# Row normalization by absolute sum: loads and stores on two queues, the last tile in halves, one broadcast multiply per tile

## The chip, the cores and the metric

The kernel runs on one core of a Trainium2 chip. The metric is the device time of the whole kernel in microseconds; the time before is the median of 8 runs. A profiled execution of the same kernel gives the busy times, waits and transfers that this document reads. Engines are named as in the profile: DVE is VectorE, ACT is ScalarE, POOL is GpSimd, SP is SyncE, and "SPq" is SP's queue of DMA issues.

## The reference

The input is 32 x 512 x 1024 in f32, that is 16384 rows of 1024. Each row is divided by the sum of its absolute values:

```python
def reference(x):
    sums = np.sum(np.abs(x), axis=-1, keepdims=True)
    return (x / (sums + 1e-8)).astype(np.float32)
```

67.1 MB are read and 67.1 MB are written, and nothing is used twice.

## The kernel before

The 16384 rows are cut into 8 tiles of 2048 rows. In a tile each of the 128 partitions holds R = 16 whole rows that lie one behind the other in memory, so a tile is 128 x 16 x 1024 f32: 64 KB per partition, 8.39 MB in all. The pool `sbuf` has three buffers for `x_tile`, so three tiles can be on the chip at a time, and a tile is computed in place: the buffer that was loaded is also the one that is stored, and it is free for the next load when its store has landed.

For each tile one DMA loads it (line 66, on SP's queue). `process_chunk` then works on a number of rows per partition: VectorE sums the absolute values along each row (`tensor_reduce`, line 37) and takes the reciprocal (line 45). The rows are then multiplied by their reciprocals one instruction per row, the first `mv` rows by VectorE (`tensor_scalar_mul`, line 48), the others by ScalarE (`activation` with a scale, line 54). The chunk is then stored by a DMA on SP's queue too (line 60).

The first six tiles are one chunk of 16 rows, with 10 rows on VectorE and 6 on ScalarE. The last two tiles are loaded whole but computed and stored in four chunks of 4 rows, with 2 rows on each engine; these stores are 2 MB each.

Loads and stores stand in one queue, SP's, and the tile framework's scheduler decides their order. In the trace it is: loads of tiles 0, 1, 2; stores of 0, 1, 2; loads of 3, 4, 5; stores of 3, 4, 5; loads of 6 and 7; the eight 2 MB stores. A store that waits for its rows holds up the loads behind it on SP. On VectorE the scheduler interleaves the chunks of the last two tiles.

Of the kernel before, what the change touches and what calls it, by code (L numbers as in the profile page):

```python
# [1 line left out]

# [4 lines left out]


@with_exitstack  # L10
def kernel(
    ctx: ExitStack,
    tc: tile.TileContext,
    x: bass.AP,
    out: bass.AP,
):
    nc = tc.nc
    P = nc.NUM_PARTITIONS

    x_flat = x.flatten_outer_dims()  # L20
    out_flat = out.flatten_outer_dims()
    n, d = x_flat.shape

    R = 16
    assert n % (P * R) == 0
    ntiles = n // (P * R)

    x_t = x_flat.rearrange("(n p r) d -> n p r d", p=P, r=R)
    out_t = out_flat.rearrange("(n p r) d -> n p r d", p=P, r=R)

    BUFS = 3
    sbuf = ctx.enter_context(tc.tile_pool(name="sbuf", bufs=BUFS))
    stats = ctx.enter_context(tc.tile_pool(name="stats", bufs=BUFS))

    def process_chunk(x_tile, out_ap, r0, rN, mv):
        s = stats.tile([P, rN], mybir.dt.float32, tag="s")
        nc.vector.tensor_reduce(  # L37
            out=s[:, :],
            in_=x_tile[:, r0 : r0 + rN, :],
            axis=mybir.AxisListType.X,  # L40
            op=mybir.AluOpType.add,
            apply_absolute_value=True,
        )
        inv = stats.tile([P, rN], mybir.dt.float32, tag="inv")
        nc.vector.reciprocal(out=inv[:, :], in_=s[:, :])  # L45
        for r in range(rN):
            if r < mv:
                nc.vector.tensor_scalar_mul(  # L48
                    out=x_tile[:, r0 + r, :],
                    in0=x_tile[:, r0 + r, :],  # L50
                    scalar1=inv[:, r : r + 1],
                )
            else:
                nc.scalar.activation(  # L54
                    out=x_tile[:, r0 + r, :],
                    in_=x_tile[:, r0 + r, :],
                    func=mybir.ActivationFunctionType.Copy,
                    scale=inv[:, r : r + 1],
                )
        nc.sync.dma_start(out=out_ap[:, r0 : r0 + rN, :], in_=x_tile[:, r0 : r0 + rN, :])  # L60

    MV = 10

    for i in range(ntiles):
        x_tile = sbuf.tile([P, R, d], x.dtype)
        nc.sync.dma_start(out=x_tile[:, :, :], in_=x_t[i, :, :, :])

        if i < ntiles - 2:
            process_chunk(x_tile, out_t[i], 0, R, MV)
        else:  # L70
            C = 4
            for c0 in range(0, R, C):
                process_chunk(x_tile, out_t[i], c0, C, (MV * C) // R)


# [1 line left out]
_INS = ['x']  # L77
_OUTS = [((32, 512, 1024), 'float32')]


# [23 lines left out]
```

## Time and profile before

| | |
|---|---|
| median of 8 runs | 318.69 us (318.1 to 319.26) |
| profiled execution | 319.0 us |
| its span on the core | 317.2 us |
| VectorE busy | 190.8 us, 60% of the span |
| ScalarE busy | 56.6 us, 18% |
| HBM read and written | 67.11 MB each, 423 GB/s over the span |
| DMA packets | 3170, of which 352 under 512 B |
| VectorE waited for loads | 111.5 us, 3 times |

Times in the profile are counted from the start of the span. The share of a DMA queue is the time that its packets took on the core's 16 DMA engines, as a share of 16 engines' span. A transfer's "time to landing" runs from the start of its issue on the queue to the last of its 16 completion marks, so it includes the transfers that stand ahead of it in the queue. "Idle before" of a group is the time that the engine stood still just before the group's instructions, with what ended it.

### The profile page before, as it was taken

The page shows a single profiled execution, that of the slowest core. Times are in us where ns is not written, and L with a number is a line of the kernel's source. Part 1 is how long each engine was busy: PE and PEld are TensorE (multiplying, and loading weights), DVE is VectorE, ACT ScalarE, POOL GpSimd, SP SyncE. Part 2 cuts the span into 40 slices and gives each one's busy share as a digit, 9 for nine tenths or more (in the row PEclk, how much of TensorE's full clock was granted, in tenths as well). Part 3 has the DMA queues.
Part 4 walks back from the last instruction along what each step waited for, and adds up shares of the span by engine and source line. Part 5 has one row for each costly group of instructions (what it writes and reads, how often), then busy time and mean ns, then how long its engine had stood idle before and what let it go on. Part 6 is the DMA issues. An engine that isn't in the chain of part 4 may idle for free.

```text
span 317.2 us, 261 instructions
## 1 busy us (share of the span) xinstructions
DVE 190.8 (60%) x104; ACT 56.6 (18%) x53; POOL 0.2 (0%) x4
## 2 busy tenths in 40 slices
DVE  0019999999990000039999999980000069999920
ACT  0010080080080000000070070080000002522520
POOL 0000000000000000000000000000000000000000
DMA  9999999999999999999999999999999999999797
GB/s 388 405 397 471 455 397 405 388 438 479 405 397 521 405 397 430 488 405 397 512 413 397 397 480 438 405 438 471 413 397 479 438 405 438 390 433 430 326 430 331
DMA packets 3170, 134.24 MB, mean 423 GB/s; under 512 B 352, under 2 KB 352, under 8 KB 352
## 3 DMA queue, kind: packets, MB, share of 16 engines
q1 hardware_dynamic: 3168, 134.22, 98.5%
q14 instruction: 2, 0.02, 0.0%
HBM read 67.11 MB, written 67.11 MB: 423 GB/s over the span
## 4 chain that ended last, share of the span: by engine, by line
DVE 56%; DMA 35%; issue 4%; ACT 0%; ACTq 0%; SPq 0%; DVEq 0%
DVE s L37 41%; DMA x_tile<-in_x_dram 35%; DVE x_tile L48 15%; DVE inv L45 1%; ACT x_tile L54 0%; ACTq L99 0%; SPq L60 0%; DVEq L45 0%; DVEq L48 0%
## 5 line engine op out<-in xcount | busy, mean ns | idle before, releaser
L37 DVE TENSOR_REDUCE s<-x_tile 128x4 f32<-128x4096 f32 (+1 forms) x14 | 138.3, 9892 | 111.5 <-DMA x_tile<-in_x_dram 111.5
L54 ACT ACTIVATE x_tile<-x_tile,inv 128x1024 f32<-128x1024 f32 x52 | 55.4, 1137 | 224.1 <-DVE inv L45 224.1
L48 DVE TENSOR_SCALAR x_tile<-x_tile,inv 128x1024 f32<-128x1024 f32 x76 | 51.4, 747 | 0.3
L54 ACT ACT_TABLE_LOAD x1 | 1.3, 1283 | 23.0 <-DMA x_tile<-in_x_dram 23.0
L45 DVE RECIPROCAL inv<-s 128x4 f32<-128x4 f32 (+1 forms) x14 | 2.7, 202 | 0.4
L88 POOL MEMSET const-bfloat16-1.0<- 128x1 bf16 x1 | 0.1, 101 | 0.0
L88 POOL MEMSET const-uint8-127<- 128x1 uint8 x1 | 0.1, 101 | 0.0
L88 POOL MEMSET const-float32-0.0<- 128x1 f32 x1 | 0.1, 98 | 0.2 <-issue 0.2
L88 POOL MEMSET const-float32-1.0<- 128x1 f32 x1 | 0.1, 98 | 0.0
## 6 DMA issues: line engine op xcount, KB each, us to landing
out_dram<-x_tile SPq DMA_DIRECT2D x8, 2048.0 KB, 9.9
x_tile<-in_x_dram SPq DMA_DIRECT2D x8, 51.1
out_dram<-x_tile SPq DMA_DIRECT2D x6, 29.7
```

Source lines behind the costliest of these rows:

```text
L37: nc.vector.tensor_reduce(out=s[:, :], in_=x_tile[:, r0 : r0 + rN, :], axis=mybir.AxisListType.X, op=mybir.AluOpType.add, apply_absolute_v ...
L45: nc.vector.reciprocal(out=inv[:, :], in_=s[:, :])
L48: nc.vector.tensor_scalar_mul(out=x_tile[:, r0 + r, :], in0=x_tile[:, r0 + r, :], scalar1=inv[:, r : r + 1],)
L54: nc.scalar.activation(out=x_tile[:, r0 + r, :], in_=x_tile[:, r0 + r, :], func=mybir.ActivationFunctionType.Copy, scale=inv[:, r : r + 1],)
L88: nc = _bacc.Bacc("TRN2", target_bir_lowering=False, num_devices=1)
```

## The change

- All stores are issued from ScalarE's queue instead of SP's; loads stay on SP's.
- The loop is put under `manual_schedule`: every engine's instructions keep the order in which the program writes them.
- Tiles 0 to 6 are one chunk of 16 rows. Only the last tile is cut, into two halves of 8 rows, and its load is cut as well; the second-last tile is no longer cut.
- VectorE multiplies half of a chunk's rows (8 of 16, or 4 of 8) by one `tensor_mul`, whose second operand is `inv` broadcast along the row; ScalarE has the other half, one instruction per row as before.
- A step of VectorE adds 1e-8 to the sums ahead of the reciprocal.
- The pool `stats` has four buffers instead of three.

```diff
-    BUFS = 3
     sbuf = ctx.enter_context(tc.tile_pool(name="sbuf", bufs=BUFS))
-    stats = ctx.enter_context(tc.tile_pool(name="stats", bufs=BUFS))
+    stats = ctx.enter_context(tc.tile_pool(name="stats", bufs=4))
 
-    def process_chunk(x_tile, out_ap, r0, rN, mv):
+    def normalize(x_tile, r0, k, kv):
...
+        nc.vector.tensor_scalar_add(out=s[:, :k], in0=s[:, :k], scalar1=EPS)
+        inv = stats.tile([P, R], FP32)
+        nc.vector.reciprocal(out=inv[:, :k], in_=s[:, :k])
+        nc.vector.tensor_mul(
+            out=x_tile[:, r0 : r0 + kv, :],
+            in0=x_tile[:, r0 : r0 + kv, :],
+            in1=inv[:, :kv].unsqueeze(2).to_broadcast([P, kv, d]),
+        )
+        for r in range(kv, k):
+            row = x_tile[:, r0 + r, :]
+            nc.scalar.activation(
+                out=row,
+                in_=row,
+                func=mybir.ActivationFunctionType.Copy,
+                scale=inv[:, r : r + 1],
+            )
+
+    with tc.manual_schedule():
+        for i in range(ntiles):
+            parts = 2 if i == ntiles - 1 else 1
+            k = R // parts
+            x_tile = sbuf.tile([P, R, d], FP32)
+            for r0 in range(0, R, k):
+                nc.sync.dma_start(
+                    out=x_tile[:, r0 : r0 + k, :], in_=x_t[i][:, r0 : r0 + k, :]
                 )
...
+            for r0 in range(0, R, k):
+                normalize(x_tile, r0, k, k // 2)
+                nc.scalar.dma_start(
+                    out=out_t[i][:, r0 : r0 + k, :], in_=x_tile[:, r0 : r0 + k, :]
                 )
...
-        nc.sync.dma_start(out=out_ap[:, r0 : r0 + rN, :], in_=x_tile[:, r0 : r0 + rN, :])
```

On the engines this gives: VectorE runs reduce, add, reciprocal and multiply of one tile after the other, with no interleaving of chunks. ScalarE runs eight rows and a store issue for each tile, and four rows and a store issue for each half of the last. SP issues only the loads; from the fourth on, each waits until the store of the tile that had its buffer has landed.

More of the change, by code (lines that the diff above doesn't have):

```diff
@@ L7 @@
 from concourse._compat import with_exitstack
+FP32 = mybir.dt.float32
+EPS = 1e-8
 @with_exitstack
@@ L26 @@
     ntiles = n // (P * R)
+    BUFS = 3
     x_t = x_flat.rearrange("(n p r) d -> n p r d", p=P, r=R)
     out_t = out_flat.rearrange("(n p r) d -> n p r d", p=P, r=R)
-    BUFS = 3
     sbuf = ctx.enter_context(tc.tile_pool(name="sbuf", bufs=BUFS))
-    stats = ctx.enter_context(tc.tile_pool(name="stats", bufs=BUFS))
-    def process_chunk(x_tile, out_ap, r0, rN, mv):
-        s = stats.tile([P, rN], mybir.dt.float32, tag="s")
+    stats = ctx.enter_context(tc.tile_pool(name="stats", bufs=4))
+    def normalize(x_tile, r0, k, kv):
+        s = stats.tile([P, R], FP32)
         nc.vector.tensor_reduce(
-            out=s[:, :],
-            in_=x_tile[:, r0 : r0 + rN, :],
+            out=s[:, :k],
+            in_=x_tile[:, r0 : r0 + k, :],
             axis=mybir.AxisListType.X,
@@ L43, in process_chunk @@
         )
[L44 to L51, printed above, removed]
-                )
[L53 to L58, printed above, removed]
-                )
@@ L60, in process_chunk @@
[L60 to L73, printed above, removed]
+        nc.vector.tensor_scalar_add(out=s[:, :k], in0=s[:, :k], scalar1=EPS)
```

## The prediction

> **What bounds the kernel now.** I read the page first (busy shares, the DMA row, the chain), then the groups kept apart by shape, then the issue of every transfer and its time to landing, one window at a time.
>
> ```profile
> DMA  9999999999999999999999999999999999999797
> q1 hardware_dynamic: 3168, 134.22, 98.5%
> DVE 56%; DMA 35%; issue 4%; ACT 0%; ACTq 0%; SPq 0%; DVEq 0%
> ```
>
> The chain names VectorE for 56% of the span, and that misleads. The chain goes back through what each instruction waited for last, and while VectorE works on a tile the queue behind it is full all the same: the 16 DMA engines are at nine tenths in all slices but two of the last three, 98.5% over the span. The kernel moves 134.2 MB in 317.2 us. So time goes or comes only where the DMA engines idle or slow down, and where the last transfer lands.
>
> To see how evenly they run I take issue plus time to landing for single transfers (first fence: issue start and its duration; second: the same transfers' time to landing, in the same order).
>
> ```profile
> 0.73 0.38 SPq L66 DMA_DIRECT2D x_tile<-in_x_dram  x1
> 1.64 0.42 SPq L66 DMA_DIRECT2D x_tile<-in_x_dram  x1
> 47.29 0.35 SPq L60 DMA_DIRECT2D out_dram<-x_tile  x1
> 95.98 0.52 SPq L66 DMA_DIRECT2D x_tile<-in_x_dram  x1
> 120.92 0.33 SPq L66 DMA_DIRECT2D x_tile<-in_x_dram  x1
> 164.61 0.34 SPq L60 DMA_DIRECT2D out_dram<-x_tile  x1
> 213.47 0.81 SPq L66 DMA_DIRECT2D x_tile<-in_x_dram  x1
> 303.80 0.33 SPq L60 DMA_DIRECT2D out_dram<-x_tile  x1
> ```
>
> ```profile
> x_tile<-in_x_dram SPq DMA_DIRECT2D x1, 22.2
> x_tile<-in_x_dram SPq DMA_DIRECT2D x1, 61.2
> out_dram<-x_tile SPq DMA_DIRECT2D x1, 34.9
> x_tile<-in_x_dram SPq DMA_DIRECT2D x1, 44.2
> x_tile<-in_x_dram SPq DMA_DIRECT2D x1, 58.7
> out_dram<-x_tile SPq DMA_DIRECT2D x1, 34.3
> x_tile<-in_x_dram SPq DMA_DIRECT2D x1, 43.4
> out_dram<-x_tile SPq DMA_DIRECT2D x1, 2048.0 KB, 12.5
> ```
>
> Write Lk and Sk for load and store of tile k. The sums: L0 lands at 22.9, L2 at 62.8, S0 at 82.2, L3 at 140.2, L5 at 179.6, S3 at 198.9, L6 at 256.9, the last quarter of S7 at 316.3. From S3 to L6 lie three transfers (S4, S5, L6) in 58.0 us: 19.33 us each, 434 GB/s, for loads and stores alike, and S0 to L3 gives the same (58.0 for three). This is the clean price of 8.39 MB. Against it the trace loses: 1.2 us between L0 and L2 (39.9 for two), 0.7 between L3 and L5 (39.4 for two), and 1.3 behind L7, which lands at 276.3 (issued at 218.3; the two loads of that stretch have a median of 50.7, so 58.0 for it): 40.0 for the last two stores instead of 38.7. Sum: 22.9 + 15 x 19.33 + 3.2 = 316.1, measured 316.3; the span ends 0.9 later. The floor with these rows is 22.9 + 290.0 = 312.9, so 3.4 us are to be had at most.
>
> The 1.3 at the end has a place: S7's second quarter is issued at 300.20, when the first quarter's (issued at 294.43, 6.3 to landing) lands at 300.7, so the queue runs dry for about a microsecond.
>
> **The change, part by part.** Engine prices come from these groups:
>
> ```profile
> L37 DVE TENSOR_REDUCE s<-x_tile 128x16 f32<-128x16384 f32 x6 | 103.3, 17214 | 67.6 <-DMA x_tile<-in_x_dram 67.6
> L54 ACT ACTIVATE x_tile<-x_tile,inv 128x1024 f32<-128x1024 f32 x52 | 55.4, 1137 | 224.1 <-DVE inv L45 224.1
> L48 DVE TENSOR_SCALAR x_tile<-x_tile,inv 128x1024 f32<-128x1024 f32 x76 | 51.4, 747 | 0.3
> L45 DVE RECIPROCAL inv<-s 128x16 f32<-128x16 f32 x6 | 1.5, 253 | 0.4
> ```
>
> *Broadcast multiply.* Ten per-row multiplies (6.72 us per tile in the timeline) go; one 128x8192 instruction with two operands comes. No row shows it. Below: the rate of the per-row form, 8 x 0.747 = 6.0 us. Above: two operands read one after the other at the reduce's 17.214/16384 = 1.05 ns per element, 17.2 us. I take one element per 1.05 ns, 8.6 us, since the reduce is the nearest long f32 row. ACT has eight rows instead of six: six took 6.35, so eight take 8.5, level with VectorE. The added epsilon step is a 128x16 instruction; I price it as the reciprocal, 0.25. A tile then takes 17.2 + 0.25 + 0.25 + 8.6 = 26.3 us on VectorE, before 24.2. Cover: a load and a store together need 38.7 us of the DMA engines, so VectorE has some 12 us to spare per tile; without that cover the edit costs 2.1 per tile.
>
> *Two queues and program order.* Loads stay on SP's queue, stores go to ACT's. ACT's instruction order becomes eight rows, store, eight rows, store; the store issue waits for VectorE's multiply (level with the rows) and takes about 0.34, and behind it stand only the next tile's rows, which wait for a later reciprocal anyway. SP no longer queues loads behind stores: L3 now waits only for S0 to land, L4 for S1. With both queues full I let them share equally and walk it: tile 0 is done at 22.9 + 26.4 = 49.3, S0 starts while L2 has 12.3 us left; L2 lands near 72, S0 near 81, which releases L3. From then each 38.7 us bring one load and one store: loads land near 121.5, 160, 199, 237.5, the halves of L7 near 257 and 276; stores near 118, 156, 195, 234, 272. A store is issued 26.4 after its load lands (148, 187, 225, 264), some 8 us before the store ahead of it is done, so the store queue doesn't run dry, and while L7 is under way neither do the loads.
>
> *Last tile in halves.* The halves are computed from 264 to 277 and from 277 to 291. Behind L7 (276) the queue holds S6 until 294 and S7's first half until 303; the second half has been issued at 291, 12 us ahead of its turn. The dry spot of before goes, and with it the 2 MB stores: the 1.3. End: 312.9, if the 1.2 and 0.7 go as well; 314.9 if they stay.
>
> *Mixed traffic.* This is the unknown. From 49 to 276, 227 us, loads and stores are in flight together; before they never were, except at changes from one to the other. What the trace shows of changes: from store to load (S2 to L3, S5 to L6) 19.3 each, no cost. From load to store, the excess lies in the stretch just ahead: 1.2 (L0 to L2), 0.7 (L3 to L5), 0 (L6 to L7: 19.4). If these are prices of changes, they matter: a transfer is 128 packets (3168 less 352 small ones, over 22 transfers), 8 per DMA engine, 2.42 us each; if the engines alternate packet by packet, 5 packets of L2 and 40 of L3 to L7 make 45 changes from load to store. Ends: 0, and 45 x 1.2 = 54 us. A gain is excluded beyond the 3.4, because the clean stretches run at one rate whatever their direction, which points at the DMA engines themselves. I take none beyond the 1.9 already there, because the three shrink (1.2, 0.7, 0), which looks like a first touch rather than a price for each change.
>
> The Trainium skill, "DMA: Bandwidth & Descriptors", under "Issuing engines are not separate DMA queues", speaks against the change: transfers from any issuing engine run on the same 16 DMA engines, so a second queue saves only issue time. The 98.5% row agrees with that; by it alone only the 1.3 at the end is to be had. The same page, under "Latency and other measured facts", gives 214 GB/s per direction as the full rate of copies on the sync and scalar queues, 428 in sum; no run here shows mixed traffic, and if that were its rate, 227 us would grow by 1.4%, 3.2 us, and an estimate by that page ends at 320.6.
>
> **Sum.** Of the 3.4 I take the 1.3 at the end and leave the rest. Profiled execution: 319.0 - 1.3 = 317.7. The median of the runs before is 0.3 below the profiled one, so 318.69 - 1.3 = 317.4.
>
> **Rivals.**
>
> *Mixing costs at each change (slower).* Place: each DMA engine, from 49 to 276. At the mean of the three seen changes, 0.63, 45 of them give 28 us: 346. At 0.2 each, 9 us: 326. It decides from 1.3/45 = 0.03 us per change, barely over 1% of a packet, and that is why it weighs much. For it: 1.2 and 0.7 directly ahead of two of the three changes. Against it: the third shows none, and the two from store to load show none.
>
> *The multiply is at the upper end (slower).* At 17.2 a tile takes 34.9. Walked the same way, VectorE goes from tile to tile nearly without rest, the last half is done at 313 and its store lands near 325: 12 later, 329. It decides from about 11: tiles 0 and 1 run back to back and S1 is issued at 76, 5 us ahead of S0's landing at 81, so some 2 us more per tile than I take are free. Against it: 1.05 ns per element in the reduce.
>
> *The queues share unequally.* If stores get two thirds, loads come late, the store queue empties first and the tail bares VectorE: one to ten microseconds. If loads are favoured, nothing changes.
>
> *All bubbles go (faster by more).* 318.69 - 3.4 = 315.3.
>
> **How the numbers follow.** No change is within 0.2% here (0.64 us, about what a measurement of this kernel can tell): 318.05 to 319.33. My forecast with all bubbles going as its lower end: 0.56, of which 0.46 faster and 0.10 within 0.2%. Mixing: 0.35, of which 0.03 within 0.2%, the rest slower, half of that above 326. The multiply: 0.05, slower. Sharing: 0.04, slower. Sum: 0.46, 0.13, 0.41. The range goes from 315.0 (the floor's 315.3, less the spread of the runs) to 329, which takes in mixing up to about 0.26 per change and the dear multiply; what lies above is near 0.15. The forecast's own range is 315.0 to 319.3.
>
> **What would show it.** Right: the two queues together at 98.5% or more; loads landing 38.7 apart; the multiply near 8.6 us; the last store issued some 10 us before the store ahead of it lands. Wrong: 39.5 or more between loads with a full queue (mixing); a DMA row below nine in the middle or at the end (starved queue); VectorE waiting for nothing between tiles (multiply).

## The result, and the profile after

The changed kernel takes 320.35 us (median of 13 runs) where the kernel before takes 318.44 (35 runs on the same chips): the ratio is 1.0051, 95% interval 1.0043 to 1.0060. It became slower by half a per cent. The forecast was 317.4, so the sign was wrong. Medians here are of all runs, while ratios leave out runs more than 1.5% above the fastest of the same kernel: two of these 13 (324.27 and 324.62), and three of the six of loads_halved below, the profiled one among them. The profiled execution took 320.15 us with a span of 318.4.

The page of the changed kernel, for the row and the queues that were shown of before (columns of a queue: packets, MB, share of 16 engines):

```profile
DMA  9999999999999999999999999999998999999985
q1 hardware_dynamic: 1296, 67.11, 49.5%
q10 hardware_dynamic: 1296, 67.11, 48.8%
```

q1 is SP's queue with the loads, q10 ScalarE's with the stores. Together they are busy for 98.3%, as much as the one queue was. So the kernel is still bound by its transfers. What is lost shows at the end: the row of before had its weak slices there too, now the last two are 8 and 5.

The engines' groups, kept apart by shape:

```profile
L40 DVE TENSOR_REDUCE s<-x_tile 128x16 f32<-128x16384 f32 x7 | 120.5, 17218 | 82.7 <-DMA x_tile<-in_x_dram 82.7
L50 DVE TENSOR_TENSOR x_tile<-x_tile,inv 128x8192 f32<-128x8192 f32 x7 | 60.8, 8692 | 0.5
L47 DVE TENSOR_SCALAR s<-s 128x16 f32<-128x16 f32 x7 | 1.2, 175 | 0.2
```

The broadcast multiply takes 8.69 us, the epsilon step 0.18: 26.4 us from tile to tile, as forecast. VectorE waits 82.7 us for loads of whole tiles, so it isn't the bound.

Now the end, in the timeline (start, duration, what; in brackets the idle time before it and what ended it):

```profile
241.36 17.22 DVE L40 TENSOR_REDUCE s<-x_tile 128x16 f32<-128x16384 f32 x1 [12.61 <-DMA x_tile<-in_x_dram]
268.70 8.69 DVE L40 TENSOR_REDUCE s<-x_tile 128x8 f32<-128x8192 f32 x1 [0.84 <-DMA x_tile<-in_x_dram]
290.88 8.69 DVE L40 TENSOR_REDUCE s<-x_tile 128x8 f32<-128x8192 f32 x1 [8.54 <-DMA x_tile<-in_x_dram]
304.56 0.34 ACTq L75 DMA_DIRECT2D out_dram<-x_tile  x1
```

The forecast had L6 at 237.5, the halves of L7 at 257 and 276 and the last store at 291. L6 is 4 us late, but the halves are late by 12 and 15. VectorE stands still for 8.5 us ahead of the last half, and its store is issued at 304.56. What the DMA engines did meanwhile, in windows (columns: length; VectorE, ScalarE and GpSimd busy with instructions; TensorE clock; DMA share; GB/s):

```profile
52.00:235.00 183.00, 128.65 (x20) 42.11 (x40) 0.00 (x0) 1.00 0.99 429
303.00:306.00 3.00, 1.47 (x1) 1.31 (x2) 0.00 (x0) 1.00 0.59 251
```

From 52 to 235 loads and stores are side by side at a share of 0.99, 429 GB/s. Around 304 there is a dry spot: 0.41 x 3 = 1.2 us. Then the last store:

```profile
out_dram<-x_tile ACTq DMA_DIRECT2D x1, 4096.0 KB, 12.9
```

It lands at 317.5. Half a tile needs 9.7 us at 19.33 per tile, and before showed about 1.5 us ahead of that (6.3 for 2 MB issued to an empty queue, of which 4.8 are transfer): 11.2. So 1.7 us are lost in the last store too. Ahead of it lies the late load half, as the transfers from 284 to 290 show:

```profile
q10 hardware_dynamic: 40, 2.62, 100.8%
q1 hardware_dynamic: 4, 0.10, 3.8%
```

The load queue moves 0.10 MB in 6 us, three packets of 32 KB and a completion mark. Most of the 16 engines have finished L7; a few still hold its last packets, each between two 64 KB packets of the store queue, and the tile counts as landed only when the last of them is done.

The trace doesn't name the engine of a packet, but joined end to start the packets make 16 chains, one for each engine. In them thirteen engines had their last packet of L7 done at 279.1 to 280.5, three at 287.3 to 288.1. These three were 2 to 3 us behind already: two of them since L6, whose 16 completion marks lie between 237.8 and 241.0, one by store packets of up to 3.1 us from 246 to 258. Then most engines ran out of stores from 262 to 272, until S6's packets came, and moved eight or nine load packets alone; the three, still at S5, had only six. Each load packet that was left stood between two store packets and took 3.6 us instead of 1.2. In the last store too, thirteen engines are done at 315.2, three at 316.3 to 317.1.

### The profile page after: what moved, and what is told of

It is laid out like the page before. It is cut to its first block, busy times and chain, and to the rows that moved or that the text cites. A ratio compares the mean times of both kernels' runs of the same rounds, so it can differ in the third digit from the quotient of the medians.

```text
span 318.4 us, 198 instructions
## 1 busy us (share of the span) xinstructions
DVE 211.2 (66%) x36; ACT 68.8 (22%) x65; POOL 0.2 (0%) x4
## 4 chain that ended last, share of the span: by engine, by line
DMA 59%; DVE 33%; another core or an unknown queue 3%; issue 0%; SPq 0%; DVEq 0%; ACTq 0%
DMA x_tile<-in_x_dram 31%; DMA out_dram<-x_tile 28%; DVE s L40 22%; DVE x_tile L50 11%; DVE inv L49 0%; DVE s L47 0%; SPq L70 0%; DVEq L50 0%; ACTq L75 0%
## 5 line engine op out<-in xcount | busy, mean ns | idle before, releaser
L40 DVE TENSOR_REDUCE s<-x_tile 128x16 f32<-128x16384 f32 (+1 forms) x9 | 137.9, 15322 | 92.1 <-DMA x_tile<-in_x_dram 92.1
L57 ACT ACTIVATE x_tile<-x_tile,inv 128x1024 f32<-128x1024 f32 x64 | 67.5, 1135 | 212.8 <-DVE inv L49 212.8
L50 DVE TENSOR_TENSOR x_tile<-x_tile,inv 128x8192 f32<-128x8192 f32 (+1 forms) x9 | 69.7, 7744 | 0.6
L49 DVE RECIPROCAL inv<-s 128x16 f32<-128x16 f32 (+1 forms) x9 | 2.2, 241 | 0.3
L47 DVE TENSOR_SCALAR s<-s 128x16 f32<-128x16 f32 (+1 forms) x9 | 1.6, 174 | 0.3
```

The lines of the kernel that those rows point to most:

```text
L40: nc.vector.tensor_reduce(out=s[:, :k], in_=x_tile[:, r0 : r0 + k, :], axis=mybir.AxisListType.X, op=mybir.AluOpType.add, apply_absolute_v ...
L47: nc.vector.tensor_scalar_add(out=s[:, :k], in0=s[:, :k], scalar1=EPS)
L49: nc.vector.reciprocal(out=inv[:, :k], in_=s[:, :k])
L50: nc.vector.tensor_mul(out=x_tile[:, r0 : r0 + kv, :], in0=x_tile[:, r0 : r0 + kv, :], in1=inv[:, :kv].unsqueeze(2).to_broadcast([P, kv, d]),)
L57: nc.scalar.activation(out=row, in_=row, func=mybir.ActivationFunctionType.Copy, scale=inv[:, r : r + 1],)
```

## The experiments

Four theories stand in the expectations. A: the queues take turns packet by packet, so the smaller packet gets fewer bytes, and the halved load came late for that. B: each change between load and store costs on every engine. C and D: in mixed traffic single DMA engines fall behind and a transfer lands with the slowest of 16 (C said so of the tail, D for traffic as such). E: the computing engines' own traffic does it. Ratios are to the kernel before, with 95% intervals.

**store_halves.** In the changed kernel:

```diff
-                nc.scalar.dma_start(
-                    out=out_t[i][:, r0 : r0 + k, :], in_=x_tile[:, r0 : r0 + k, :]
-                )
+                piece = 8 if i in (5, 6) else k
+                for q0 in range(r0, r0 + k, piece):
+                    nc.scalar.dma_start(
+                        out=out_t[i][:, q0 : q0 + piece, :], in_=x_tile[:, q0 : q0 + piece, :]
+                    )
```

> The changed kernel with the stores of tiles 5 and 6 issued as two DMAs of 8 rows, so that their packets are 32 KB like those of the last tile's loads. Theory A (the two queues take turns packet by packet, so that a 32 KB load packet beside a 64 KB store packet gets a third of the bytes): the halves of the last load land near 257 and 277 us instead of 269 and 291, the last store is issued near 292 instead of 305, the dry spot behind it goes, the last landing is near 314 to 315.5 and the time about 2 to 3 us below the changed kernel's (317.0 to 318.3; ratio to before 0.995 to 1.000). Theory B (each change between a load and a store costs): more packets, more changes, nothing won: 320 or more. Theory C (single DMA engines lag in mixed traffic whatever the packets): the second half still lands past 285 and the time stays within 1 us of the changed kernel's.

Measured: 319.62 us, 1.0029 (1.0014 to 1.0044). The timeline of its end, and two windows:

```profile
266.49 8.68 DVE L40 TENSOR_REDUCE s<-x_tile 128x8 f32<-128x8192 f32 x1
280.08 8.69 DVE L40 TENSOR_REDUCE s<-x_tile 128x8 f32<-128x8192 f32 x1
293.75 0.34 ACTq L77 DMA_DIRECT2D out_dram<-x_tile  x1
```

```profile
303.00:306.00 3.00, 0.00 (x0) 0.00 (x0) 0.00 (x0) 1.00 1.14 492
313.00:317.00 4.00, 0.00 (x0) 0.00 (x0) 0.00 (x0) 1.00 0.10 41
```

With packets of one size VectorE waits for neither half, the last store is issued 11 us earlier and the dry spot is gone. Theory A is right on the late load; C had it past 285. But the time fell by only 0.7 us of the 2 to 3 expected, and the intervals of the two kernels just touch: from 313 to 317 a tenth of the DMA engines' time is still at work. Most engines are done at 313.5, a few end up to 3 us later. So C's forecast of the landing failed, but single late engines, its mechanism, are what is left.

**load_whole.** In the changed kernel, the last tile loaded by one DMA:

```diff
-            for r0 in range(0, R, k):
-                nc.sync.dma_start(
-                    out=x_tile[:, r0 : r0 + k, :], in_=x_t[i][:, r0 : r0 + k, :]
-                )
+            nc.sync.dma_start(out=x_tile[:, :, :], in_=x_t[i])
```

> The changed kernel with the last tile loaded by one DMA (64 KB packets); computing and storing stay in halves. Theory A: equal shares bring the whole tile at 277 to 278 us, 13 us ahead of the second half in the changed kernel, but its first half can't start before that either; the last store is issued near 304 to 305, hardly earlier than 304.6, a dry spot of about 1 us stays, the last landing is near 315.5 to 316.5 and the time 0.5 to 2 us below the changed kernel's. Theory B: one change less, the same time as the changed kernel. Theory C: the tile lands past 285, the last store is issued past 311 and the time is 323 or more.

Measured: 321.31 us, 1.0085 (1.0058 to 1.0112), from 319.67 to 323.03 between runs; the profiled run was the fastest.

```profile
278.70 8.69 DVE L40 TENSOR_REDUCE s<-x_tile 128x8 f32<-128x8192 f32 x1 [11.97 <-DMA x_tile<-in_x_dram]
305.93 0.34 ACTq L72 DMA_DIRECT2D out_dram<-x_tile  x1
```

The tile lands when A says, 12 us ahead of the changed kernel's second half. But the first half has to wait for it too, and the last store is issued later by 1.4 us. In the median the time rose by 1 us where A had it fall by 0.5 to 2; the profiled run itself was 0.5 us below the changed kernel's, so its trace doesn't show where the median's microsecond goes. Landing times follow packet sizes; the time does not follow them alone.

**loads_halved.** In the changed kernel, `k` replaced by 8 in the loop of loads, so every load has 32 KB packets.

> The changed kernel with every tile's load issued as two DMAs of 8 rows (32 KB packets), stores of tiles 0 to 6 whole. Theory A: beside a store every load gets a third: tile 2 lands near 84 us instead of 73, tile 3 near 138 instead of 124, and the phases of loads and stores drift apart, with loads waiting for nothing to share with at other times; the last half lands near 275 to 280, the last landing 314.5 to 317, the time 0 to 3 us below the changed kernel's. Theory B: the number of changes grows and the time with it, above 321. Theory C: landings like the changed kernel's (tile 2 near 73, tile 3 near 124).

Measured: 333.07 us in the median of six runs, from 328 to 340; the ratio, 1.037 (1.0328 to 1.0411), rests on the three from 328.1 to 332.1. The profiled run took 334.07, so the sizes read from it belong to a run above the median. The first reduces of tiles 2, 3 and 6, and a window of the end:

```profile
78.92 17.22 DVE L40 TENSOR_REDUCE s<-x_tile 128x16 f32<-128x16384 f32 x1 [3.52 <-DMA x_tile<-in_x_dram]
143.29 17.22 DVE L40 TENSOR_REDUCE s<-x_tile 128x16 f32<-128x16384 f32 x1 [37.93 <-DMA x_tile<-in_x_dram]
264.35 17.22 DVE L40 TENSOR_REDUCE s<-x_tile 128x16 f32<-128x16384 f32 x1 [38.55 <-DMA x_tile<-in_x_dram]
272.00:292.00 20.00, 19.84 (x5) 8.42 (x8) 0.00 (x0) 1.00 0.37 157
```

In the changed kernel tile 3 starts at 123.4 and tile 6 at 241.4; here they are 20 and 23 us later. Loads do get less beside stores of double packet size, as A has it. The time was missed by some 10 us even in the three faster runs: with unequal packets the DMA engines also drift further apart (the 16 marks of a load come to lie up to 14 us apart in the trace), and VectorE, held up until 264, then sets the end. While it works on tile 6 the DMA engines run dry for 0.63 x 20 = 12.6 us.

**two_queues_only.** In the kernel before:

```diff
-        nc.sync.dma_start(out=out_ap[:, r0 : r0 + rN, :], in_=x_tile[:, r0 : r0 + rN, :])
+        nc.scalar.dma_start(out=out_ap[:, r0 : r0 + rN, :], in_=x_tile[:, r0 : r0 + rN, :])
```

> The kernel before with one edit: stores are issued on ScalarE's queue instead of SP's. Per-row multiplies, the last two tiles loaded whole and stored in quarters, and the scheduler's order stay. Theory A: packets are 64 KB on both sides until tile 6, mixing costs nothing, the last tile lands near 276 us and the last quarter's store is issued near 304 behind a full queue: last landing 314 to 315.5, time 316.5 to 318.0, ratio to before 0.994 to 0.999. Theory B (a cost for each change between load and store): slower than before by 1 us or more, as the changed kernel is. Theory C: slower, through a late last load.

Measured: 320.19 us, 1.0065 (1.0041 to 1.0089): this one line costs as much as the whole change. Its last store has no dry spot ahead of it, but a window near 250 stands out:

```profile
293.15 0.34 ACTq L60 DMA_DIRECT2D out_dram<-x_tile  x1
out_dram<-x_tile ACTq DMA_DIRECT2D x1, 2048.0 KB, 24.0
249.00:254.00 5.00, 5.00 (x6) 1.47 (x2) 0.00 (x0) 1.00 1.04 341
```

It is issued 24 us before it lands, behind a full queue, and still lands at 317.2. Theory A fails here; what is lost is in the mixed traffic itself. Part of it has a place: from 249 to 254 the engines are all busy, but at 341 GB/s. Here S6's first quarter comes after some 14 us of loads alone, and on every engine the last load packet ahead of it takes 0.8 to 1.6 us longer than 2.42. The engines also end apart: the marks of the last store spread over 2.4 us.

**copy_one_queue** and **copy_two_queues.** Traffic alone, in place of `process_chunk` and the loop, under `manual_schedule` (for two queues: stores on `nc.scalar`, and loads 3 to 7 placed one behind each store):

```python
for what, i in order:   # L0 L1 L2 S0 S1 S2 L3 L4 L5 S3 S4 S5 L6 L7 S6 S7
    if what == "L":
        tiles[i] = sbuf.tile([P, R, d], x.dtype, tag="x_tile", name="x_tile")
        nc.sync.dma_start(out=tiles[i][:, :, :], in_=x_t[i, :, :, :])
    else:
        nc.sync.dma_start(out=out_t[i], in_=tiles[i][:, :, :])
```

> Traffic alone: the same eight loads and eight whole-tile stores of 8.39 MB in the order of the kernel before (L0 L1 L2 S0 S1 S2 L3 and so on), all on SP's queue; the reduction, the reciprocal and the multiply are left out, x is stored as it came. Nothing waits for a computation, so the queue is never dry: 22.9 + 15 x 19.33 + 1.2 (first change to stores) + 0.4 = 314.4 for the last landing, span 315.3, time 317 (ratio to before 0.995), and the 16 completion marks of a transfer lie within 2 us. All theories agree here; it is the base for the next run.

> The same traffic alone with stores on ScalarE's queue, loads on SP's, 64 KB packets on both sides; the computation is left out as in the run on one queue. Theory D (mixed traffic holds up single load packets of single DMA engines by 0.1 to 1 us, and a transfer lands with the slowest of 16): the median engine ends like on one queue plus a dry spot of 1.5 us ahead of the last store, but marks of one transfer come to lie 2 to 5 us apart and the time is 2 to 5 us above the run on one queue. Theory E (the drift comes from the computing engines' traffic beside the DMA, not from mixing): marks within 2 us as on one queue, time above it only by the dry spot, 1.5 us.

Measured: 316.78 us (0.9948, 0.9934 to 0.9961) on one queue, 320.64 (1.0066, 1.0053 to 1.0080) on two. No engine computes in either, so theory E falls: 3.9 us come from the two queues' traffic alone. Windows of the copy on two queues, then its queues from 290 to 296 and the issue of its last store:

```profile
140.00:290.00 150.00, 0.00 (x0) 1.00 1.00 433
290.00:297.00 7.00, 0.00 (x0) 1.00 0.45 197
```

```profile
q10 hardware_dynamic: 33, 1.25, 48.0%
q1 hardware_dynamic: 5, 0.13, 5.1%
```

```profile
296.24 0.34 ACTq L43 DMA_DIRECT2D out_dram<-x_tile  x1
```

Up to 290 the mixed traffic runs at 433 GB/s, just as the copy on one queue does in the same window. Then the DMA engines stand half idle for 7 us: thirteen have their last packet of L7 by 286.8, but in 6 us the load queue moves two more packets (0.13 MB) on two late engines, and S7 can't be issued until they have landed. The 16 marks of L7 run from 288.8 to 295.9; in the copy on one queue those of a transfer lie at most 1.4 us apart. In the chains of packets these two engines had, after the start, load packets of 2.5 to 3.3 us among the usual 2.42, some 4 us too many on each; a third had 2 us, the other thirteen at most 0.5.

**copy_same_direction** and **copy_alternating** ask whether two queues or two directions do it. The first cuts every transfer in two halves, one on each queue, in the order of the copy on one queue; the second keeps one queue and whole tiles, in the order L0 L1 L2 S0 S1 L3 S2 L4 S3 L5 S4 L6 S5 L7 S6 S7.

```diff
+    queues = ((nc.sync, 0), (nc.scalar, R // 2))
...
+            for q, r0 in queues:
+                half = tiles[i][:, r0 : r0 + R // 2, :]
```

> Traffic alone, no computation (x is stored as it came), in the order L0 L1 L2 S0 S1 S2 L3 and so on, but every transfer is cut in two halves of 8 rows, one on SP's queue and one on ScalarE's: both queues are busy all the time, yet loads meet stores only at the changes of direction. Theory D1 (loads and stores side by side hold up single packets): like the copy on one queue, 316.5 to 318. Theory D2 (two queues as such let the DMA engines drift apart): like the copy on two queues, 319.5 to 321.

> Traffic alone, no computation (x is stored as it came), one queue, whole tiles, but loads and stores alternate: L0 L1 L2 S0 S1 L3 S2 L4 S3 L5 S4 L6 S5 L7 S6 S7, six changes from load to store instead of three. If every such change cost the 1.1 us of the first one, three more of them give 320; if only the first store costs it and later ones 0 to 0.4, the time is within 1 us of the copy in groups of three, 316.5 to 318. Theory D1 too says 316.5 to 318, since directions follow one another and are not side by side.

Measured: 317.48 us (0.9964, 0.9949 to 0.9979) with both queues in one direction, 319.00 (1.0001, 0.9980 to 1.0021; 317.0 to 319.4 between runs) on one queue that alternates. Two busy queues cost little as long as they go the same way. Alternating on one queue does cost 2.2 us in the median, which neither theory had: D1 expected nothing, and 1.1 us for each of three more changes would have given 320. The window of its end:

```profile
313.00:317.00 4.00, 0.00 (x0) 1.00 0.04 16
```

For 2.5 of these 4 us one late engine alone moves its last packets; the copy on one queue in groups has its last packets at 314.1. So it isn't the queues, and after the first change it isn't a price on all engines alike. Where a load packet is followed by a store packet on the same DMA engine, some load packets are held up; most engines lose little, one or two lose microseconds.

**changed_one_queue.** The changed kernel with stores on `nc.sync` and the queue order of before:

```diff
-                nc.scalar.dma_start(
...
+        for group in ((0, 1, 2), (3, 4, 5), (6, 7)):
...   # loads of a group, then its tiles and stores
+                    nc.sync.dma_start(
```

> The changed kernel with the stores back on SP's queue, loads and stores in the order of the kernel before (three loads, three stores); the broadcast multiply, the epsilon step and the last tile in halves stay. No mixing, so no drift of engines. But VectorE takes 26.4 us per tile: the third store of a group is ready at 22.9 + 79.2 = 102.1, after the second has landed (101.5), dry for 2 to 2.5 us, twice; tile 6 is stored whole, ready 26.4 us after its load lands, 8 to 9 us after the last load: dry again; the last half is ready near 315. Last landing near 325 to 329, ratio to before 1.03 to 1.04. If it comes out below the changed kernel, the second queue is what costs, and these dry spots are not as I read them.

Measured: 333.0 us, 1.0458 (1.0442 to 1.0474), a little above the 1.03 to 1.04 expected.

```profile
99.00:105.00 6.00, 3.14 (x1) 2.87 (x3) 0.00 (x0) 1.00 0.42 175
219.00:226.00 7.00, 3.65 (x1) 3.38 (x4) 0.00 (x0) 1.00 0.36 150
281.00:292.00 11.00, 10.84 (x5) 8.42 (x8) 0.00 (x0) 1.00 0.34 144
```

The three dry spots lie where they were expected. From the windows they come to 3.5, 4.5 and 7.3 us (rough, since packets are 2.4 us long), about 15 together, as much as the kernel lies above before. So on one queue the rest of the change costs far more than the second queue does, and this run doesn't price the second queue.

**multiply_only.** In the kernel before, `MV = 8` and

```diff
+        nc.vector.tensor_mul(
+            out=x_tile[:, r0 : r0 + mv, :],
+            in0=x_tile[:, r0 : r0 + mv, :],
+            in1=inv[:, :mv].unsqueeze(2).to_broadcast([P, mv, d]),
+        )
```

> The kernel before with one edit: VectorE multiplies half of a chunk's rows (8 of 16, 2 of 4) by one broadcast multiply, ScalarE the other half; one queue, the scheduler's order, the last two tiles in quarters. VectorE's 26.2 us per tile instead of 24.2 make the third store of a group ready at 22.9 + 78.6 = 101.5, when the second has landed: dry for 1.5 to 2.5 us in each of two groups; each quarter takes 0.7 us longer, so the last one is issued near 312 to 316 behind an empty queue and lands near 320 to 324. Time 322 to 327, ratio to before 1.01 to 1.03. If the multiply is hidden: within 0.3% of before.

Measured: 329.81 us, 1.0349 (1.0322 to 1.0377); more than expected.

```profile
99.00:105.00 6.00, 2.24 (x1) 1.97 (x2) 0.00 (x0) 1.00 0.82 350
219.00:226.00 7.00, 2.18 (x1) 1.92 (x2) 0.00 (x0) 1.00 0.70 300
298.00:312.00 14.00, 14.00 (x7) 6.20 (x6) 0.00 (x0) 1.00 0.63 266
176.00:182.00 6.00, 6.00 (x1) 0.00 (x0) 0.00 (x0) 1.00 0.97 350
```

The three dry spots (first three lines) come to 1.1, 2.1 and 5.2 us, 8.4 together, of which before has 2 (see the next run). So they explain some 6 of the 11 us. Some 3 more lie in long packets: from 176 to 182 the engines are busy but move 350 GB/s, and the last load packet ahead of the store takes 0.5 to 1.4 us longer on every engine, as near 58. On one queue with three loads ahead of three stores, VectorE has no 12 us to spare per tile: three tiles stand in a row behind each group of loads. Under the changed order the same multiply is hidden.

**in_order_tail.** In the kernel before, `manual_schedule` and the queue order written out; nothing else:

```diff
-    for i in range(ntiles):
+    with tc.manual_schedule():
+        for group in ((0, 1, 2), (3, 4, 5), (6, 7)):
...
+            for i in group:
+                C = R if i < ntiles - 2 else 4
```

> The kernel before with one edit: program order instead of the scheduler's (the queue order of loads and stores stays the same), so VectorE finishes each quarter of the last two tiles before it begins the next. One queue, no mixing. The dry spots of before lie at 294 and 300 us, ahead of the first two quarters of the last tile, about 1.9 us together: a quarter takes 4.4 + 0.2 + 1.5 = 6.1 us, so the last tile's quarters are issued near 288, 294, 300 and 306 instead of 294, 300, 302 and 304. With theory A and D alike: the two dry spots go, the last quarter comes about when its turn comes (310), last landing 314.5 to 316, time 0.5 to 1.9 us below before (ratio 0.994 to 0.998). If the last quarter's issue at 306 plus its own 6 to 7 us decides: at least 313, so it does not.

Measured: 317.60 us, 0.9973 (0.9962 to 0.9984), faster than both kernels. The end, first this kernel's, then the same window of before:

```profile
290.00:304.00 14.00, 13.58 (x11) 4.93 (x5) 0.00 (x0) 1.00 1.01 431
```

```profile
290.00:304.00 14.00, 12.97 (x13) 7.41 (x7) 0.00 (x0) 1.00 0.86 366
```

The dry spots of before, 0.14 x 14 = 2 us, are gone; they lie ahead of S7's first quarter as well as its second, the one that the prediction named. What is left above the copy on one queue is 0.8 us.

## Why the prediction was wrong

**Right.** The bound: the queues together at 98.3%, a little under the 98.5% forecast. The multiply at 8.69 us against 8.6, and 26.4 per tile. The walk up to tile 5, within 4 us: L3, L4 and L5 let their reduces start at 123.4, 163.6 and 202.3 (forecast 121.5, 160, 199). That L2 landed near 72 (its last mark is at 71.9) is luck: equal shares from 49.3 on would give 49.3 + 2 x 12.3 = 73.9. That the multiply is hidden under the changed order: the change is no slower than its second queue alone.

**The step that failed first** is "I take none beyond the 1.9 already there, because the three shrink (1.2, 0.7, 0), which looks like a first touch". The price of mixing was put as one number for all engines, and at nothing. For the median engine of the copies and of the changed kernel it is indeed next to nothing after the first change: 433 GB/s in the mixed copy, 434 in the clean stretches. But a transfer lands with the slowest of 16, and single engines lose 2 to 4 us over the mixed stretch. The sign that was named for mixing, 39.5 us or more between loads, shows it: from L3 to L4 the first marks lie 38.6 us apart, the last marks 39.9. Traffic alone costs 3.9 us on two queues, of which some 3 are the wait for the late engines ahead of the last store; in the kernel of before the one edited line costs 1.6 to 2.1. That is the rival "mixing costs at each change" with a wrong shape: place right, price paid mostly by a few engines. In the mixed copy its break-even of 0.03 us per change was passed not on average but by the slowest. Nor was it a first touch: in two_queues_only every engine pays 0.8 to 1.6 us near 250, in multiply_only 0.5 to 1.4 near 178, long after the first store.

**The second** is "With both queues full I let them share equally", carried on to the halves of the last tile. A half has packets of 32 KB, the store beside it 64, and the queues take turns by packets. So beside a store the load got a third. Most engines finished the second half at 279 to 280; the three that were late already fell 8 us behind. So the half came at 291 instead of 276, and "The dry spot of before goes, and with it the 2 MB stores: the 1.3" failed: a dry spot of 1.2 came back. The rival of unequal sharing had this mechanism and got a chance of 0.04; that the change itself halves the packets stood in the diff. The Trainium skill, "DMA: Bandwidth & Descriptors", "Queues, rings and completion order", says that each engine alternates between its queues at packet granularity. The runs agree: equal packets brought the second half 11 us forward, halved loads came 20 us late.

**The sum.** The profiled execution missed 317.7 by 2.45 us. The dry spot is 1.2 of it and the last store 1.7, by three late engines; together 2.9, and about half a microsecond came back elsewhere, which I can't place.

**The page's estimate** of 320.6 lies close to what was measured, but by luck, for another reason. The mixed stretch runs at 429 to 433 GB/s, not visibly below the clean rate; the time goes in waits for late engines. Nor did the rule on issuing engines that the prediction cites warn of that: it has transfers of all queues share the same engines, which they do, but here the second queue cost time instead of saving none.

**Open.** What makes a load packet ahead of a store packet long on one engine and not on the next isn't shown. Nor is why before loses 1.2 and 0.7 us on all engines at two of its three changes: "first touch" was my guess, and the packets near 250 and 178 speak against it, but no run shows what makes one change dear and another free.

## What to carry to other kernels

When a kernel is bound by transfers, ask of a second queue which directions it puts side by side, not only whether it keeps the engines full: a transfer ends with the slowest DMA engine, and the queue's mean rate hides that. Queues share by packets, so cutting one side's transfers changes who gets the bytes. Before parts are moved to another queue, look for the dry spots in the queue there is; here putting the last quarters in order gained 0.9 us, where the second queue lost 1.6 or more.

## What the runs showed of the hardware that I had not expected

- Eight loads and eight stores of 8.39 MB take 316.8 us on one queue in groups of three, 317.5 on two queues that go the same way, 319.0 on one queue that alternates, and 320.6 on two queues that go opposite ways.
- With load packets of 32 KB beside store packets of 64 KB, the loads of tiles 3 and 6 came 20 and 23 us later than with equal packets (in a run of 334.07 us), and the ratio to before rose from 1.005 to 1.037.
- A load packet of 64 KB takes 2.42 us, but the last one ahead of a store can take 0.5 to 1.6 us longer on all 16 engines at once (multiply_only near 178, two_queues_only near 250), or next to nothing (before near 273).
- A multiply of 128x8192 f32 whose second operand is broadcast takes 8.69 us, as long as the reduce of 128x8192 with its one operand.
